# A channel shuffle on one core: the 16 KB tile moves from third place to the end

## The chip, the cores and the metric

One core of one Trainium2 chip. The metric is the device time of one execution in microseconds (us). "Before" and "changed" were timed in turns on the same chip; all runs quoted are of the fast state unless a run is called slow. A spread of some tenths of a us between runs is normal here; among fast runs of the kernel before it reached 1.5 us once (316.22 to 317.76).

## The reference

```python
batch, h, w, c = 16, 64, 64, 256        # float32, groups = 8
x = x.reshape(batch, h, w, groups, channels_per_group)
x = x.transpose(0, 1, 2, 4, 3)          # within each row of 256 channels: (8, 32) -> (32, 8)
x = x.reshape(batch, h, w, c)
```

67.1 MB go in, 67.1 MB come out, and each row of 256 channels (1 KB) is permuted within itself. The arithmetic is nothing; the kernel is a copy through the core.

## The kernel before

512 units of 128 rows (one 1 KB row for each of 128 partitions, 131,072 B) are cut into tiles. A tile of size 38 puts 38 KB into each partition. SP issues the loads, VectorE (DVE) copies with the permuted access pattern, ACT issues the stores. Two buffers hold loaded tiles and three hold copied ones.

```python
_SLOTS = [[4, 8, 16], [28]] + [[38]] * 12     # tiles of one slot share one buffer
_IN_BUFS = 2
_OUT_BUFS = 3
# ... cut: pools, rows(flat, first, q) = the DRAM rows of a tile of size q
for parts in _SLOTS:
    in_tile = in_pool.tile([P, biggest * c], F32, name="in_tile")
    out_tile = out_pool.tile([P, biggest * c], F32, name="out_tile")
    # ... cut: pieces = (size, first row, columns) of each part
    for q, start, cols in pieces:
        nc.sync.dma_start(out=in_tile[:, cols], in_=rows(x_flat, start, q))
    for q, start, cols in pieces:
        nc.vector.tensor_copy(
            out=out_tile[:, cols].rearrange("p (i j g) -> p i j g", j=CPG, g=G),
            in_=in_tile[:, cols].rearrange("p (i g j) -> p i j g", g=G, j=CPG),
        )
        nc.scalar.dma_start(out=rows(out_flat, start, q), in_=out_tile[:, cols])
```

A load needs the buffer that the copy two slots earlier has read, so the load of slot i+2 and the store of slot i are issued at the same event, the end of copy i.

## Time and profile before

| | before |
|---|---|
| time, median of 3 runs | 316.23 us (316.10 to 316.65) |
| span in the profile | 314.7 us |
| bytes moved by DMA | 134.22 MB, mean 427 GB/s |
| VectorE busy | 119.4 us, 38% |

The lines of the profile stand in the prediction. One more view is needed here, the issues with their median time from issue to landing, loads first:

```profile
in_tile<-in_x_dram SPq DMA_DIRECT2D x12, 4864.0 KB, 37.0
out_dram<-out_tile ACTq DMA_DIRECT2D x12, 4864.0 KB, 48.3
```

A tile of 38 alone would need 11.5 us at 434 GB/s. That it takes 37 us in and 48 us out says that transfers stand in line. The stores stand longer: a new store finds older ones ahead of it.

### The profile page before, as it was taken

To read this page: it belongs to the slowest core of one execution; us is meant where nothing else is said; L and a number is where in the kernel's file an instruction comes from. 1 tells how busy PE (TensorE), PEld (TensorE's weight loads), DVE (VectorE), ACT (ScalarE), POOL (GpSimd) and SP (SyncE) were. 2 spreads that over 40 slices of the span, in tenths; PEclk is the share of its full clock that TensorE was granted. 3 is DMA by queue.
4 is the path that set the end of the run, shared out by engine and by line. 5 is a ranking of instruction groups with operands and counts; after the bars stand their busy time and mean duration, and the time that the engine had idled before them with its cause. 6 is when DMAs were issued, how large, how long until landed. Compare 5 with 4: busy or idle time off the path is not lost.

```text
span 314.7 us, 131 instructions
## 1 busy us (share of the span) xinstructions
DVE 119.4 (38%) x16; POOL 0.2 (0%) x4
## 2 busy tenths in 40 slices
DVE  3417090730911901902803804604605506407300
POOL 0000000000000000000000000000000000000000
DMA  8999999999999999999999999999999999999997
GB/s 314 421 427 469 381 417 442 442 449 401 470 401 470 401 470 401 465 406 445 425 440 430 435 435 425 445 401 470 396 475 396 470 401 470 401 470 401 470 401 317
DMA packets 4608, 134.22 MB, mean 427 GB/s; under 512 B 512, under 2 KB 512, under 8 KB 768
## 3 DMA queue, kind: packets, MB, share of 16 engines
q1 hardware_dynamic: 2304, 67.11, 49.8%
q10 hardware_dynamic: 2304, 67.11, 49.4%
HBM read 67.11 MB, written 67.11 MB: 427 GB/s over the span
## 4 chain that ended last, share of the span: by engine, by line
DMA 74%; DVE 19%; SPq 0%; issue 0%; DVEq 0%
DMA in_tile<-in_x_dram 74%; DVE out_tile L57 19%; SPq L55 0%; DVEq L57 0%
## 5 line engine op out<-in xcount | busy, mean ns | idle before, releaser
L57 DVE COPY out_tile<-in_tile 128x9728 f32<-128x9728 f32 (+4 forms) x16 | 119.4, 7463 | 174.7 <-DMA in_tile<-in_x_dram 174.7
L80 POOL MEMSET const-bfloat16-1.0<- 128x1 bf16 x1 | 0.1, 102 | 0.0
L80 POOL MEMSET const-uint8-127<- 128x1 uint8 x1 | 0.1, 102 | 0.0
L80 POOL MEMSET const-float32-0.0<- 128x1 f32 x1 | 0.1, 99 | 0.2 <-issue 0.2
L80 POOL MEMSET const-float32-1.0<- 128x1 f32 x1 | 0.1, 99 | 0.0
## 6 DMA issues: line engine op xcount, KB each, us to landing
in_tile<-in_x_dram SPq DMA_DIRECT2D x12, 4864.0 KB, 37.0
out_dram<-out_tile ACTq DMA_DIRECT2D x12, 4864.0 KB, 48.3
in_tile<-in_x_dram SPq DMA_DIRECT2D x1, 3584.0 KB, 21.0
out_dram<-out_tile ACTq DMA_DIRECT2D x1, 3584.0 KB, 37.1
in_tile<-in_x_dram SPq DMA_DIRECT2D x1, 2048.0 KB, 11.1
out_dram<-out_tile ACTq DMA_DIRECT2D x1, 2048.0 KB, 30.2
in_tile<-in_x_dram SPq DMA_DIRECT2D x1, 1024.0 KB, 5.2
out_dram<-out_tile ACTq DMA_DIRECT2D x1, 1024.0 KB, 21.5
```

The costliest lines, as they stand in the source:

```text
L57: nc.vector.tensor_copy(out=out_tile[:, cols].rearrange("p (i j g) -> p i j g", j=CPG, g=G), in_=in_tile[:, cols].rearrange("p (i g j) -> ...
L80: nc = _bacc.Bacc("TRN2", target_bir_lowering=False, num_devices=1)
```

## The change

The intent is a quick start and a short finish: the tile that is stored last has less than half the size, so its copy and its store, which nothing follows, are shorter.

```diff
-_SLOTS = [[4, 8, 16], [28]] + [[38]] * 12
+_SLOTS = [[4, 8], [28]] + [[38]] * 12 + [[16]]
```

## The prediction

> **What bounds the kernel now.** I read the page first: the busy times, the 40 slices, the chain, the costliest groups. One execution spans 314.7 us.
>
> ```profile
> DVE 119.4 (38%) x16; POOL 0.2 (0%) x4
> DVE  3417090730911901902803804604605506407300
> DMA  8999999999999999999999999999999999999997
> DMA packets 4608, 134.22 MB, mean 427 GB/s; under 512 B 512, under 2 KB 512, under 8 KB 768
> DMA 74%; DVE 19%; SPq 0%; issue 0%; DVEq 0%
> L57 DVE COPY out_tile<-in_tile 128x9728 f32<-128x9728 f32 (+4 forms) x16 | 119.4, 7463 | 174.7 <-DMA in_tile<-in_x_dram 174.7
> ```
>
> The reader is to see two things that seem to disagree. The chain of waits alternates DMA (74%) and the DVE copy (19%), as if the 8.8 us copies were part of the bound. But the row of DMA digits is 9 in 38 of 40 slices, and DVE is idle 62% of the time, always waiting for a load. A chain of waits shows which event released which; it does not show whether the shared DMA engines ever ran out of work. The digits say that they did not. So I cut the span into stretches and read the DMA share and rate of each (columns: stretch, length, DVE and POOL busy, clock, DMA share, GB/s; a packet's bytes count where it starts, so short stretches swing):
>
> ```profile
> 0.00:2.00 2.00, 0.00 (x0) 0.20 (x4) 1.00 0.22 45
> 2.00:10.00 8.00, 3.13 (x2) 0.00 (x0) 1.00 1.00 390
> 10.00:34.00 24.00, 10.47 (x2) 0.00 (x0) 1.00 1.03 441
> 34.00:38.00 4.00, 0.00 (x0) 0.00 (x0) 1.00 0.87 324
> 38.00:285.00 247.00, 96.97 (x11) 0.00 (x0) 1.00 1.01 434
> 289.00:312.00 23.00, 5.11 (x1) 0.00 (x0) 1.00 1.00 433
> 313.50:314.70 1.20, 0.00 (x0) 0.00 (x0) 1.00 0.00 0
> ```
>
> From 38 to 285 us the DMA engines move 434 GB/s without a break, and in the tail, where no load is left, 433 GB/s. This rate is the limit. Work it out: 134.22 MB / 434 GB/s = 309.3 us. The span is 5.4 us longer, and the losses are: before the first packets, 2.0 x (1 - 45/434) = 1.8 us; from 2 to 10 us, 8 x (1 - 390/434) = 0.8 us; from 34 to 38 us, 4 x (1 - 324/434) = 1.0 us, of which the stretch before gives 0.4 back (441 against 434); after the last packet 1.2 us; the rest, about 1 us, is rounding of the rates and the packets that straddle a cut. There is no hole of the size of a copy anywhere, least of all at the end.
>
> The timeline gives the two edges, and the issues give the time to landing:
>
> ```profile
> 3.97 1.11 DVE L57 COPY out_tile<-in_tile 128x1024 f32<-128x1024 f32 x1 [3.97 <-DMA in_tile<-in_x_dram]
> 6.42 2.02 DVE L57 COPY out_tile<-in_tile 128x2048 f32<-128x2048 f32 x1 [1.33 <-DMA in_tile<-in_x_dram]
> 12.76 3.88 DVE L57 COPY out_tile<-in_tile 128x4096 f32<-128x4096 f32 x1 [4.31 <-DMA in_tile<-in_x_dram]
> 23.09 6.59 DVE L57 COPY out_tile<-in_tile 128x7168 f32<-128x7168 f32 x1 [6.45 <-DMA in_tile<-in_x_dram]
> ...
> 262.29 8.81 DVE L57 COPY out_tile<-in_tile 128x9728 f32<-128x9728 f32 x1 [14.13 <-DMA in_tile<-in_x_dram]
> 285.28 8.83 DVE L57 COPY out_tile<-in_tile 128x9728 f32<-128x9728 f32 x1 [14.19 <-DMA in_tile<-in_x_dram]
> ```
>
> ```profile
> out_dram<-out_tile ACTq DMA_DIRECT2D x1, 4864.0 KB, 19.7
> ```
>
> The last load lands just before 285.28 us. The last copy ends at 294.1, its store of 38 lands 19.7 us later. But 38 x 128 KB = 4.98 MB alone would take 11.5 us at 434 GB/s: for the other 8 us this store stood behind older stores. That backlog is what hides the last copy.
>
> **What the Trainium skill says.** "DMA: Bandwidth & Descriptors", Specifications, gives a fabric ceiling of 435 GB/s for the 16 DMA engines of a core; the trace agrees, 434 over 247 us, so loads and stores together sit at the ceiling. The same page, "Queues, rings and completion order", says that each DMA engine goes round the queues that have work, one packet at a time, and that loads from SP and stores from ACT are two such queues. The trace agrees in kind: with equal 38 KB rows, the two queues took 49.8% and 49.4%, and the small stores of the start took 12.5 us (512 KB) and 21.5 us (1024 KB) to land, because each of their short packets waits for a long load packet. The consequence here is that the order of sizes changes who goes first, while the total rate stays, as long as either queue has work. "SBUF — State Buffer", "SBUF: two separate sides", says that engine accesses cannot slow DMA; no loss shows here beside copies, since DVE is busy 97.0 of the 247 us at 434 GB/s.
>
> **The change part by part.** No byte, packet, copy or issue is added or removed: the same 16 loads, copies and stores; in the order of each of SP, DVE and ACT one entry moves from third to last. There is one slot more, 15 for 14. A unit of size (128 KB, 131,072 B) costs 131,072 / 434 GB/s = 0.302 us of DMA.
>
> Start. The loads of 4 and 8 and their copies stay where they are (8 is copied from 6.42 to 8.44). The load of 28 follows at once, and lands at the earliest at 6.4 + 28 x 0.302 = 14.9 us, or 18.5 if the stores of 4 and 8 (12 x 0.302 = 3.6) get all their turns before it. The first load of 38 no longer waits for the copy of 16 (ended at 16.64) but for that of 8, so it is issued at 8.5 instead of 16.7 us, 6 to 10 us before the load ahead of it is done. It lands at 26.4 to 30.0. The second 38 needs the copy of 28, done at 14.9 + 6.6 = 21.5 to 25.1: 4.9 us before the queue of loads would run dry. From then on a load of 38 takes at least 38 x 0.302 = 11.5 us and a copy 8.8, so the next is issued 2.7 us before the queue is empty even if loads have the DMA alone. Cost of the start: 0 us. Removed on DVE: the idle 4.3 us before the copy of 16 and that copy, both beside full DMA: gain 0.
>
> Tail. Let T be the landing of the twelfth 38. Before, the stores then outstanding were (313.5 - 285.3) x 434 = 12.2 MB, 93 units: the twelfth and the eleventh tile and 17 units of the tenth. I take the same backlog here, plus the load of 16, in all 109 units, 33 us of DMA work. The twelfth copy takes 8.8 us; work that doesn't depend on it is 17 + 38 + 16 = 71 units, 21.4 us: covered. If the load of 16 takes turns with 38 KB store packets, 16 KB against 38 KB, it lands (16 + 38) x 0.302 = 16.3 us after T; its copy (3.9 us) ends at T + 20.2. By then 67 of 109 units are done, 42 are left, 16 of them its own store, so 26 units (7.9 us) still stand ahead of it: covered. It takes the output buffer of the tenth 38, whose 17 units (with 7 of the load between) are out at T + 7.3, before the twelfth copy ends. Gain of the tail: 0 us; cost: 0.
>
> Sum: 0 us. What may differ is the loss in the first 38 us (0.8 + about 0.6) and the spread at the end.
>
> **The rivals.** (a) The shorter tail pays. Read off the chain, the last copy falls from 8.83 to 3.88 us (-4.95) and the last store from 38 to 16 units (-6.6): 316.2 - 11.6 = 304.6 us. For it: both stand last in the chain. Against: 433 GB/s from 289 to 312 us, so what leaves the last tile comes earlier in the same full queue. (b) The start starves. With one load less in hand, loads might wait for the copy of 28, costing up to its 6.6 us: 322.8 us. For it: stores are scarce in the first 20 us, so loads must fill the DMA alone. Against: the 4.9 us margin above. (c) The load of 16 comes late through taking turns and the final copy and its issue lie bare: 3.9 us plus about 1 for hand-overs, 321 us. Against: 7.9 us of cover. (d) The early losses of 2 to 10 and 34 to 38 us go or double: 1 us either way, 315.2 or 317.2.
>
> **Range and chances.** The three runs before spread over 0.55 us. With a zero sum and (d) as the main uncertainty I say 316.2 us, range 315.4 to 317.2. A 2% change needs 6.3 us: only (a) gives that downward, for which I leave 0.01; (b) or an unseen gap upward, 0.02; within 2%, 0.97.
>
> **What would show it.** Right: the row of DMA digits again full to the last slice, 433 to 434 GB/s from about 38 us to the last packet, the first 38 issued near 8.5 us, DVE idle only for loads, the last copy near T + 16 us with the final store landing several us later than its own 4.8 us needs. Wrong: a stretch well under 434 GB/s between 10 and 30 us (b), or in the last 15 us (c); DVE waiting for a store in the tail (the buffer argument); a mean rate over the span well above 427 GB/s would mean that I misread where the 5.4 us go (a).

## The result, and the profile after

| | before | changed |
|---|---|---|
| median of 6 runs each | 316.34 us | 316.18 us (316.11 to 316.22) |
| span in the profile | 314.7 us | 314.4 us |

The ratio is 0.9994, with a 95% interval from 0.9981 to 1.0006. A ratio is the mean time of one kernel's fast runs over that of the other's of the same rounds, so not quite the ratio of the medians quoted. Executions over 1.5% slower than the fastest of the same kernel are left out of the means. The time is the same.

The page of the changed kernel, its lines for busy digits, bytes and the chain:

```profile
DVE  2081907309109109019028028037046055065400
DMA  7999999999999999999999999999999999999997
DMA packets 4608, 134.22 MB, mean 427 GB/s; under 512 B 512, under 2 KB 512, under 8 KB 768
DMA 76%; DVE 19%; issue 0%; SPq 0%; DVEq 0%
```

The stretches of the changed kernel (stretch, length, DVE and POOL busy, clock, DMA share, GB/s):

```profile
2.00:10.00 8.00, 3.11 (x2) 0.00 (x0) 1.00 1.04 429
10.00:34.00 24.00, 10.39 (x2) 0.00 (x0) 1.00 1.01 425
34.00:38.00 4.00, 4.00 (x1) 0.00 (x0) 1.00 0.89 385
38.00:285.00 247.00, 95.75 (x12) 0.00 (x0) 1.00 1.00 434
296.50:312.00 15.50, 1.91 (x1) 0.00 (x0) 1.00 1.01 436
```

The DMA is as full as before, at the same 434 GB/s, and up to the end: bytes count where a packet starts, so a short stretch such as the last may read a little above the rate. The early losses have moved about (429 for 390, 425 for 441, 385 for 324) and cancel as far as these stretches can show: weighting the rates by their lengths (with 23 GB/s in the first 2 us for 45), 15.22 MB had started by 38 us and 15.09 before. The difference of 0.13 MB (0.3 us) is less than one packet of 38 KB on each of 16 engines (0.62 MB), which can fall on either side of a cut.

The two edges in the timeline of the changed kernel:

```profile
16.36 6.57 DVE L57 COPY out_tile<-in_tile 128x7168 f32<-128x7168 f32 x1 [7.73 <-DMA in_tile<-in_x_dram]
30.18 8.82 DVE L57 COPY out_tile<-in_tile 128x9728 f32<-128x9728 f32 x1 [7.25 <-DMA in_tile<-in_x_dram]
...
278.19 8.73 DVE L57 COPY out_tile<-in_tile 128x9728 f32<-128x9728 f32 x1 [14.21 <-DMA in_tile<-in_x_dram]
294.54 3.87 DVE L57 COPY out_tile<-in_tile 128x4096 f32<-128x4096 f32 x1 [7.62 <-DMA in_tile<-in_x_dram]
```

and its issues, with the time to landing of the two stores that matter:

```profile
out_dram<-out_tile ACTq DMA_DIRECT2D x12, 4864.0 KB, 42.6
...
out_dram<-out_tile ACTq DMA_DIRECT2D x1, 2048.0 KB, 15.2
```

The copy of 28 ends at 22.9 us, 7.2 us before the load ahead is down, so the start does not starve. At the end the copy is indeed 5 us shorter, and the last store has 2 MB instead of 5. But that store was issued at 298.4 and took 15.2 us to land, though 2.10 MB need 4.8 us at 434 GB/s. For more than 10 us it stood behind older stores. The short finish was given to a queue that was full anyway.

### The profile page after: what moved, and what is told of

It reads as the page before. It is cut to its first block, busy times and chain, and to the rows that moved or that the text cites. A ratio compares the mean times of both kernels' runs of the same rounds, so it can differ in the third digit from the quotient of the medians.

```text
span 314.4 us, 132 instructions
## 1 busy us (share of the span) xinstructions
DVE 119.0 (38%) x16; POOL 0.2 (0%) x4
## 2 busy tenths in 40 slices
DMA packets 4608, 134.22 MB, mean 427 GB/s; under 512 B 512, under 2 KB 512, under 8 KB 768
## 4 chain that ended last, share of the span: by engine, by line
DMA 76%; DVE 19%; issue 0%; SPq 0%; DVEq 0%
DMA in_tile<-in_x_dram 76%; DVE out_tile L57 19%; SPq L55 0%; DVEq L57 0%
## 6 DMA issues: line engine op xcount, KB each, us to landing
out_dram<-out_tile ACTq DMA_DIRECT2D x12, 4864.0 KB, 42.6
out_dram<-out_tile ACTq DMA_DIRECT2D x1, 2048.0 KB, 15.2
```

## The experiments

Each ran three timed rounds beside the kernel before, on the same chip in the same call (medians of before: 316.45, 316.32, 316.31 and 316.32 us in the four calls). Theory A is the one of the prediction: the total stays as long as either queue has work. At the record's threshold of 2% only a_copy6, t18_last and t18_last_perm count as slower, starve as unclear, t4_34 has no verdict and the others count as the same; where a smaller difference is read below, it rests on an interval that leaves out 1.

**1. Take the last copy away (b_nolastcopy).** From the kernel before; wrong in the last tile.

```diff
-            nc.vector.tensor_copy(...)
+            last = first == b * h * w
+            if not last:
+                nc.vector.tensor_copy(...)
-                out=rows(out_flat, start, q), in_=out_tile[:, cols]
+                out=rows(out_flat, start, q), in_=(in_tile if last else out_tile)[:, cols]
```

> The kernel before, but its last tile (38) is stored straight from the loaded buffer, without the VectorE copy (wrong values in those rows on purpose). Theory A (the DMA engines are full to the last packet, the last copy lies beside a backlog of stores): no change, within 0.5 us of 316.3. Theory B (the chain of waits bounds the end, so the copy at its end counts): shorter by that copy, 8.8 us, 307.5.

Measured: 316.29 us, ratio 0.9991 (0.9969 to 1.0013). The last 8.8 us of VectorE in the chain are gone, and the time stays. The chain of waits names the last copy truthfully as a releaser, but it costs nothing.

**2 and 3. Lengthen the last copy (a_copy3, a_copy6).** From the changed kernel, with 3 in the one and 6 in the other.

```diff
-            nc.vector.tensor_copy(...)
+            for _ in range(3 if parts == [16] else 1):
+                nc.vector.tensor_copy(...)
```

> The changed kernel, with the last copy (16) done three times, 7.7 us more of VectorE at the very end of the chain. Theory A: the last store is issued at 298.4 + 7.7 = 306.1 us, the store ahead of it ends at 308.0 to 308.4 us in the trace of the changed kernel and the first load shows about 1 us from issue to first packet, so it is just covered: 0 to +0.5 us, 316.2 to 316.7. Theory B: +7.7 us, 323.9.

> The changed kernel, with the last copy done six times, 19.4 us more. Theory A: the last store is issued at 317.8 us, 9.4 us after the queue ran empty; with 1 us to its first packet it costs +10 to +11 us, 326 to 327.5, with a hole in the DMA from about 308.4 to 318.8 us. Theory B: +19.4 us, 335.6.

Measured: 316.19 us (ratio 0.9991, 0.9967 to 1.0015) and 326.79 us (ratio 1.0325, 1.03 to 1.0349). 7.7 us more cost nothing; 19.4 us more cost 10.3. The cover over the last copy therefore ends about 9 us further on (19.4 - 10.3), and its edge is seen in the stretches of the kernel with six copies:

```profile
300.00:308.00 8.00, 7.93 (x3) 0.00 (x0) 1.00 0.92 399
309.00:319.00 10.00, 9.41 (x3) 0.00 (x0) 1.00 0.00 0
319.00:324.00 5.00, 0.00 (x0) 0.00 (x0) 1.00 0.99 419
```

Ten microseconds with no byte moving: this is what a finish that matters would look like, and neither of the two kernels has it.

**4. An order that does starve (starve).** From the changed kernel.

```diff
-_SLOTS = [[4, 8], [28]] + [[38]] * 12 + [[16]]
+_SLOTS = [[38], [16], [4, 8], [28]] + [[38]] * 11
```

> The same tiles in another order: 38, then 16, then 4 and 8, 28, eleven of 38. Theory A (the total stays as long as either queue of DMAs has work): the loads of 38 and 16 are done at about 18 us, the copy of 38 ends at about 22 us and only then are the next load and the first store issued, so a hole of about 5 us from 18 to 23 us and +4.5 to +5.5 us, 320.7 to 321.7. Theory C (only the bytes count, the order of the tiles never matters): 316.2, within 0.5 us.

Measured: 322.68 us, ratio 1.0193 (1.0166 to 1.0221). Its stretch with the hole:

```profile
19.00:25.00 6.00, 6.00 (x2) 0.00 (x0) 1.00 0.07 5
```

VectorE is busy for all of it and DMA for nothing: both loads are down, and no buffer is free until the copy of 38 ends at 23.9 us. The hole is 5.9 us where 5 were expected, since the first 38 landed at 15.1 us and not at about 13.3. The total, 6.2 us above the kernel before, is likewise 1.0 us above the range of Theory A. So the order of the tiles can cost time; "only the bytes count" is wrong, and the changed kernel passes because its loads are always issued early enough.

**5. No grading at all (eq32).**

```diff
-_SLOTS = [[4, 8], [28]] + [[38]] * 12 + [[16]]
+_SLOTS = [[32]] * 16
```

> Sixteen equal tiles of 32 in place of the graded sizes: no small tile at the start, none at the end. Theory A: two loads of 32 last until about 21 us, the first copy (32/38 of 8.8 = 7.4 us) runs from about 11.7 to 19.1 us and the next load goes out before the queue of loads is empty; no hole, 316.2, from -0.5 to +1.5 us. Theory D (the small first tiles fill the pipeline and earn their place): the first copy starts about 7.7 us later than with the tile of 4, so +5 to +8 us, 321 to 324.

Measured: 316.72 us, ratio 1.0016 (0.9994 to 1.0038). Small first tiles are not needed: the first copy ends at 20.7 us, and the second load lands only at 22.9 us, so the third is issued in time.

**6 and 7. Fewer bytes at the end and at the start (a_nostore16, b_nostore16).** The same edit on the changed kernel and on the one before; those rows stay unwritten.

```diff
-            nc.scalar.dma_start(...)
+            if q != 16:
+                nc.scalar.dma_start(...)
```

> The changed kernel without the store of the tile of 16 (those rows are left unwritten on purpose), 2.10 MB less of 134.22. Theory A: 2.10 MB / 434 GB/s = 4.8 us less, 311.4. Theory B: the chain still ends with the copy of 16, 0 to -1 us of change.

> The kernel before without the store of its tile of 16 in third place (rows left unwritten on purpose). Theory A: the same 4.8 us less as at the end, 311.4: bytes weigh the same wherever they stand. Theory B: the store is 250 us ahead of the end, off the chain of loads and copies, so no change, within 0.5 us of 316.3.

Measured: 311.38 us (ratio 0.9843, 0.9827 to 0.986), 4.9 us less where the bytes say 4.8, and 313.29 us (ratio 0.9905, 0.9891 to 0.992), which is neither expectation: 3.0 us less. The trace of the second has full DMA to 296 us and then this:

```profile
38.00:296.00 258.00, 104.21 (x12) 0.00 (x0) 1.00 1.00 434
296.00:299.00 3.00, 1.54 (x1) 0.00 (x0) 1.00 0.49 208
```

The stretch loses 3 x (1 - 208/434) = 1.6 us, most of the missing 1.8. The cause proposed: while both queues have work they take turns packet by packet, each tile has 128 data packets whatever its size, and so each store is paid with one load. One store less in the third place then means that later stores stand further forward; the median store of a 38 lands after 33.0 us instead of 48.3, and at the end there is less backlog, too little for a copy of 8.8 us.

```profile
out_dram<-out_tile ACTq DMA_DIRECT2D x12, 4864.0 KB, 33.0
```

The traces give the size. From the landing of the last load on, 8.09 MB of stores still start here (11.83 MB in the kernel before, counted by the packets that start after 288.74 and 285.28 us). Without the last tile's own 4.98 MB that is 3.11 MB, 7.2 us at 434 GB/s, against 6.85 MB, 15.8 us, before. The copy of 8.8 us is covered by the second and bare for 1.6 us by the first, which is the loss seen. But the backlog fell by 3.7 MB, more than the 2.1 MB that were not stored and less than a whole tile of 38 (5.0 MB): the backlog is shown, and that it is counted strictly in turns is not.

**8. The test of that (b_nostore16_nolastcopy).** Experiment 7 with the edit of experiment 1 on top.

> The kernel before without the store of its 16 and with its last tile stored straight from the loaded buffer (both wrong on purpose). The kernel without that store alone took 313.3 us, 1.9 more than the bytes say, and its trace has a hole near 296 to 299 us, while the last copy ends. Theory A, sharpened (one store less in the queue means one tile less of backlog at the end, and the last copy is no longer covered): without the copy the hole closes, 311.4 us, 1.9 less. If the missing 1.9 us came from elsewhere (the start, the rate): 313.3, no change from taking the copy away, as it made none in the whole kernel.

Measured: 311.95 us, ratio 0.9861 (0.9846 to 0.9876), 1.3 us less than experiment 7. The same two stretches:

```profile
38.00:296.00 258.00, 96.94 (x11) 0.00 (x0) 1.00 1.00 434
296.00:299.00 3.00, 0.00 (x0) 0.00 (x0) 1.00 0.96 415
```

The hole is closed by the very edit that did nothing in experiment 1. So the copy at the end was bare there and is covered here; what decides is the backlog of stores. About 0.5 us of the 1.9 expected is not accounted for.

**9 and 10. A short tile where the backlog is thin (t18_first, t18_last).** From the changed kernel.

```diff
-_SLOTS = [[4, 8], [28]] + [[38]] * 12 + [[16]]
+_SLOTS = [[18]] + [[38]] * 13        # t18_first
+_SLOTS = [[38]] * 13 + [[18]]        # t18_last
```

> One tile of 18 and then thirteen of 38. Theory A, sharpened: each store takes turns with a load from the start; with a single short tile ahead the stores fall behind by less than two tiles, so that at the landing of the last load about 0.6 of a tile (7 us) of older stores is left, against 8.8 us of copy and 1 us to the first packet: a hole of 2 to 4 us in the tail, 318.3 to 320.3. Theory C (only the bytes count): 316.2.

> Thirteen tiles of 38 and then the one of 18. Theory A, sharpened: the last load takes turns with a store and lands late, its copy is 4.2 us, and one whole tile (11.5 us) of older stores is left: no hole in the tail; at the start the third load is issued at about 24 us, about when the second lands, a hole of at most 1 us. 316.0 to 317.5, so here the short tile at the end pays 1 to 4 us over the same tile at the start. Theory C: 316.2, the same as with it in first place. Theory D (small first tiles are needed): 11 us more, 327.

Measured: t18_first 319.74 us, ratio 1.0108 (1.0088 to 1.0129) from three fast runs (a fourth, slow, took 327.73). The same count gives 7.55 - 4.98 = 2.57 MB of older stores at the landing of the last load, 5.9 us against a copy of 8.9. The hole is where it was expected:

```profile
38.00:301.00 263.00, 103.11 (x12) 0.00 (x0) 1.00 1.00 433
301.50:304.50 3.00, 2.46 (x1) 0.00 (x0) 1.00 0.03 13
```

t18_last, which should have been better, took 330.43 us, ratio 1.0449 (1.0417 to 1.0481). The expectation was wrong by 13 us, and Theory A with it. Theory D's 327 came nearest in number, but its reason fails: the start costs little here, and experiment 5 had done without small first tiles. Its stretches:

```profile
25.00:29.00 4.00, 2.46 (x1) 0.00 (x0) 1.00 1.02 272
60.00:280.00 220.00, 80.83 (x10) 0.00 (x0) 1.00 1.00 413
```

There is a small loss at the start (4 x (1 - 272/434) = 1.5 us, in a short stretch and with the engines counted as busy, so slow packets and not a hole). No hole opens beside the last copy, but the engines finish unevenly: the last 8 us (320 to 328) run at 265 GB/s, a loss of 3.1 us, where the last 8 us of the kernel before run at 389 and lose 0.8. The main part is the rate: it is 413 GB/s, not 434, with the DMA share at 1.00. Over some 250 us this is 12 us (an estimate: 250 x (1 - 413/434)). The DMA queues of this kernel in the stretch from 60 to 280 us (q1 loads, q10 stores; packets, MB, share of the time of 16 engines):

```profile
q10 hardware_dynamic: 1311, 45.41, 52.2%
q1 hardware_dynamic: 1314, 45.53, 47.9%
```

and of the kernel before in the same stretch:

```profile
q1 hardware_dynamic: 1377, 47.98, 50.4%
q10 hardware_dynamic: 1384, 47.30, 49.7%
```

Bytes over time: an engine stores at 45.41 MB / (0.522 x 16 x 220 us) = 24.7 GB/s here and at 27.0 before; loads run at 27.0 in both. So the store packets alone are slower, by 9%. Storing by itself is not the cause, since the tail of the kernel before, only stores, runs at 433 GB/s. What may set this kernel apart is seen in its issues:

```profile
in_tile<-in_x_dram SPq DMA_DIRECT2D x13, 4864.0 KB, 39.1
out_dram<-out_tile ACTq DMA_DIRECT2D x13, 4864.0 KB, 39.3
```

Load and store are issued at the same event, the end of a copy; here they also take the same time to land, so that each load and the store two tiles older start and end almost together. This is called lockstep below. In most kernels at 433 to 434 GB/s they do not: 37.0 and 48.3 before, 37.0 and 42.6 in the changed kernel, 37.0 and 31.5 in t18_first. But eq32 is close to it, 31.1 and 32.9, and runs at 433 GB/s from 60 to 280 us with stores at 27.0 GB/s an engine. So being nearly in step is not enough, and either the last 2 us or the tile size matter, or lockstep isn't the cause.

**11. Break the lockstep (t4_34).** From t18_last: `[[4, 34]] + [[38]] * 12 + [[18]]`.

> The kernel with thirteen tiles of 38 and the 18 at the end took 330.4 us: a hole of about 2 us at the start, and then only 414 GB/s, store packets of 38 KB taking 1.57 us instead of 1.44; there each load and the store two tiles older begin and end in the same moment. Here its first tile is cut into 4 and 34 (two loads, two copies, two stores), nothing else. Theory E (the lockstep of equal load and store is what slows the stores): the store of 4 gets ahead, the stores lag a broken number of tiles, the rate is 433 to 434, no hole at the start, 316.0 to 317.0. Theory F (thirteen tiles of 38 and an 18 at the end are slow by themselves): 326 to 329.

Measured: four runs at 316.67, 329.88, 332.41 and 337.35 us; the last three count as slow. The fast one lies in the range of Theory E, the others above that of Theory F. The kernel before, timed in the same rounds, stayed between 316.16 and 316.67 us, so it was not the chip as a whole that was slow. The profile fell on the run of 329.88 us:

```profile
60.00:280.00 220.00, 79.69 (x10) 0.00 (x0) 1.00 1.00 414
...
in_tile<-in_x_dram SPq DMA_DIRECT2D x12, 4864.0 KB, 39.6
out_dram<-out_tile ACTq DMA_DIRECT2D x12, 4864.0 KB, 39.8
```

The lockstep had come back by itself, with the slow rate. The same program can run both ways. This speaks against sizes that are slow by themselves, and does not prove that the lockstep is the cause, since the fast run has no profile. It also touches experiment 10: a state is judged against the fastest run of the same kernel, so the four runs of t18_last count as fast only beside each other, and it stays open whether that program has a faster speed too. t18_first, with its one run of 327.73, may be another program of two speeds.

**12. Other addresses (t18_last_perm).** From t18_last: the same program, tiles taken from memory in another order.

```diff
-    for parts in _SLOTS:
+    for i, parts in enumerate(_SLOTS):
+        if i < 13:
+            first = P * 38 * (i // 2 + 7 * (i % 2))
+        else:
+            first = P * 38 * 13
```

> The same slow kernel of thirteen 38 and the 18, same sizes, waits and order of instructions, but the tiles are taken from memory in the order 0, 7, 1, 8, 2, 9 and so on, so that the store in flight is one tile behind the load in memory instead of two. If the slow stores come of the distance of the two addresses in HBM: another rate than 414 GB/s, at best 434 and 318 to 319.5 us. If they come of the lockstep alone or of the SBUF side: unchanged, 329.5 to 331.5 us and store packets of 1.57 us.

Measured: 332.22 us, 0.7 above the range for no effect, ratio 1.0485 (1.0454 to 1.0515), 412 GB/s from 60 to 280 us. The distance in memory between the load and the store in flight is not what slows the stores, at least not between one tile and two. Left open: why the stores run at 24.7 GB/s an engine in these kernels, whether the lockstep is the cause or goes along with it, and what brings it about in t4_34. No version tried beats the two kernels.

## Why the prediction was right, point by point

**The bound.** The DMA rate of 434 GB/s as the limit, with the copies in the chain costing nothing: shown by experiment 1 (a copy less, 0), 2 (two short copies more, 0) and 6 (2.10 MB less, 4.9 us).

**The start.** First 38 issued at 8.5 us predicted, 8.66 measured. Landing of 28 at 14.9 to 18.5, measured 16.4. Landing of the first 38 at 26.4 to 30.0, measured 30.2, just outside. Second 38 issued 4.9 us before the queue would run dry, measured 7.2. Rival (b) is real as a mechanism, as experiment 4 shows, but these sizes keep clear of it.

**The tail.** The load of 16 was to land 16.3 us after T; with T = 278.19 its copy starts at 294.54, 16.35 later, and in that stretch the trace has 144 packets of each queue (128 of data and 16 of under 512 B), 2.10 MB loaded and 4.98 MB stored: the taking of turns between 16 KB and 38 KB packets was the right model. For the small stores of the start it is only part of the reason: no store packet starts between the first issue at 5.12 us and 9.1 us, 4.0 of the 12.5 us that this store took to land. The cover was put at 26 units, 7.9 us. The last store waited 15.2 - 4.8 = 10.4 us behind others and experiments 2 and 3 give about 9 us. The term that was too small is the backlog at T, taken as 93 + 16 = 109 units from the kernel before: (313.3 - 278.2) x 434 GB/s = 15.2 MB are 116. The error lay on the safe side, which was luck. Rival (c) is excluded by the same numbers. DVE waited only for loads, never for a store, so the argument on the third output buffer held.

**Rival (a)**, 304.6 us from the chain, is refuted by the result and by experiment 1. Experiments 7 to 9 show the condition under which a shorter last copy would pay in part: a backlog of older stores that takes less time than the last copy.

**Rival (d)** and the range. The early losses did shift, with a sum too near to zero for these stretches to tell; the median moved by 0.16 us. Why the rate dips from 2 to 10 us in the one kernel and from 34 to 38 us in both was not examined.

**What the prediction took for granted** is that "the total rate stays, as long as either queue has work". It holds for these two kernels. Experiments 10 and 12, and the profiled run of 11, have work in the queues and a rate 5% lower. The prediction had nothing by which to tell such an order of sizes from this one, so that the change kept clear of it was luck; otherwise the time would have been some 13 us longer.

## What to carry to other kernels

A chain of waits that ends in a copy and a store says who released whom, not what to shorten: look first at whether the shared resource, here the DMA engines, has any empty stretch, and take the suspected link away to see whether the time moves. A short last tile can pay only if, when the last load lands, the older stores still queued are fewer bytes than the DMA would move during the last copy (no run here shows it pay); a small first tile pays only if the loads run out before the first buffer is free. Of a kernel that runs at the DMA limit, compare the rates of loads and stores too, since a full queue may still be a slow one.

## What the Trainium skill lacked or had wrong

- "DMA: Bandwidth & Descriptors", Specifications: the fabric ceiling of 435 GB/s was right for loads and stores together (434 over 247 us). No page describes what t18_last shows with both queues full: 413 GB/s over 220 us, with stores at 24.7 GB/s an engine and loads at 27.0. That load and store begin and end together there is seen; that this is the cause is not shown.
- "DMA: Bandwidth & Descriptors", "Queues, rings and completion order": the turns packet by packet are right, and they predicted a landing to 0.1 us (16.3 and 16.35). What is missing is the consequence, that transfers of unequal size shift the lag of one queue behind the other: one store of 2.1 MB less early on took the median store of a 38 from 48.3 us down to 33.0, and 3.7 MB off the backlog at the last landing.
- "DMA: Bandwidth & Descriptors", "SWDGE vs HWDGE vs iDMA", table of the descriptor pipeline: a packet is put at 4096 B preferably, there for the software path. It gives no size in bytes for the two hardware queues of this chip. Here, as the trace counts packets, 4608 moved 134.22 MB; without the 512 under 512 B, that is 32.8 KB a packet, and a short packet of one queue waits for a long one of the other.
- No page mentions two speeds of one program on a single core: 316.67 us in one run, 329.88 to 337.35 in three others of t4_34, the granted clock being 1.0 in all; t18_first has 327.73 beside 319.66 to 319.80.
